# The last projection's last 128 positions with exchanged operands, in a planned two-layer decoder on one core

## The chip, the core and the metric

The kernel runs on one core of a Trainium2 chip. Time is device time of that core in microseconds (us). The core has a matrix engine (TensorE: PE in the profile, PEld for its weight loads), a vector engine (DVE), an activation engine (ACT), a general engine (POOL) and a sync engine (SP), which here issues most DMAs; ACT issues some. Each engine works its own list in order, and waits on semaphores for the others.

## The reference

The model has width 1024, 2048 positions, two layers. What matters here is the end of the second layer and the final norm:

```python
x = x + (o * jax.nn.silu(g)) @ w_out_b[j]      # o: attention, 512 wide; w_out_b: 512 x 1024
return _rmsnorm(x, norm_f)                     # y = x * rsqrt(mean(x*x) + eps) * norm_f
```

Ahead of it stand a gated short-convolution layer, a shared key/value projection and a causal stick-breaking attention with 8 heads of 64. All of it is computed to float32 accuracy.

## The kernel before

Activations are kept transposed, channels on the 128 partitions and positions along a row: the input is `xT`, the output `outT`. The 2048 positions are worked in four chunks of 512 (`CH`), and the kernel's order of positions is reversed. Products of float32 accuracy are made of three faster ones: each operand is split into a high and a low part (`split`), and hi·hi, hi·lo and lo·hi are added up in PSUM (`mm3`). The first layer and the shared projections use a seven-product block scheme (`fast_unit`; tiles `fa`, `fd`, `fe`), the attention (`attend`) scores a band of 192 keys per 128 queries (`z`), takes a sigmoid (ACT), a mask (POOL) and a running product (DVE, a scan, `R`), transposes on PE (`wt`), splits (`wth` on ACT, `wtl` on DVE) and multiplies with the values (`av`). A second, full attention stands behind a flag and a branch at the end of the program, and is not executed for these inputs.

The last stage of a chunk c is `out_kept` for c = 0, 1, 2, and `out_last` for c = 3. The gated attention output of the chunk is `og` (4 tiles of 128 channels, hi and lo); the weights `wob` (w_out_b, hi and lo) stay in SBUF for all four chunks. For each of 8 blocks of 128 output channels (`ob`), 12 products with a block of `wob` as the stationary operand and 512 positions of `og` as the moving one make `pob`, 128 channels by 512 positions; DVE adds the residual `x` (loaded from `x1_d`), ACT squares it, and ACT multiplies by the final gain. In the last chunk the squares of blocks 0 to 4 are added on POOL (`acc`), those of blocks 5 to 7 stay apart; `add_sums` adds all up over the channels with products by a column of ones (`pst`, one column of PSUM for each 128 positions, a full float32 product). Twelve small DVE operations on four columns (`rsqrt`; tiles `v`, `t`, `yr`) make the reciprocal root, four transposes each (`bcast`; tiles `prb_x` and, for POOL, `prb_x23s`, copied to `pbs`) spread it over the partitions, and eight multiplications (six DVE, two POOL) of 128x512 are followed by eight DMAs of 256 KB to `outT`.

Nothing of the order is left to the compiler. The body is recorded (`Recorder`), each operation with its part's name, then put in one order by `order`: a list scheduler with fixed costs for each operation, which takes at each step the operation that can start first, and among equals the one with the smaller key. The keys come from the table `PLAN`: a part's name and the two ends of a stretch of due times (`m..` first layer, `po..` its output, `kq..`/`vg..` the shared projections, `aCH` attention of chunk C and head H, `gCB` the gating, `wo` the loading of `wob`, `oC`/`nC` the last projection and the norm of chunk C). So each engine's list is a result of that table. `square_into`, `rsqrt`, `bcast`, `fold_gains` (splits w_out_b once and writes it to DRAM), `keep_ob` (loads `wob`), `mm3`, `out_b` (branch not taken) and `out_last` are the places that the change touches.

## Time and profile before

| | |
|---|---|
| median of 3 runs | 1340.01 us (1339.97 to 1340.18) |
| the profiled execution | 1341.83 us, of which the profile's span holds 1340.0 us |
| PE busy / weight loads / DVE / ACT / POOL | 1302.8 / 1078.0 / 1016.9 / 599.7 / 435.5 us |
| DMA | 364.99 MB, mean 272 GB/s |
| last product of the last projection (`pob`) ends, by the chain | 1320.87 us |
| last column sum (`pst`) starts | 1324.5 us |
| last output DMA issued | 1332.5 us |

Times within the profile count from the span's start. A line number L363 (L365 after the change) is that of the function which emits the recorded operations, so all rows carry it, and the tile names tell them apart; numbers at the ends of names are left out by the profile (`x` stands for any residual tile, `og_t`, `og_b` and so on are parts of names). "Idle before" is how long the engine stood still just ahead of a group, with the engine that ended it.

### The profile page before, as it was taken

The numbers are of one execution on the slowest core, as the hardware profiler recorded it, in microseconds if no ns is written. First come the engines' busy times: TensorE is split into PE (matmuls) and PEld (weight loads), VectorE is DVE, ScalarE is ACT, GpSimd is POOL, SyncE is SP. The second block draws the span as 40 slices with busy tenths as digits, with TensorE's granted clock in tenths as the row PEclk, the third lists the DMA queues.
The fourth block names the chain that finished last, engine by engine and source line by source line (L and its number), as shares of the span: only waits on it lengthen the run. The fifth ranks groups of instructions, "written<-read, shape, count | busy, mean of one in ns | idle before, by whom it ended". The sixth has DMA issues, their size and how long they took to land.

```text
span 1340.0 us, 18973 instructions
## 1 busy us (share of the span) xinstructions
PE 1302.8 (97%) x6184; PEld 1078.0 (80%) x6184; DVE 1016.9 (76%) x1607; ACT 599.7 (45%) x1052; POOL 435.5 (33%) x553
## 2 busy tenths in 40 slices
PE   8999999999999999999999989999999999999996
PEld 6888888888888888888787777788778887788885
DVE  7899866689964655656869578877998886797855
ACT  7344534444432332323334334554555553566643
POOL 5252000001000000010032355334357675547982
PEclk9999999999999999999999999999999999999997
DMA  9439879878898799987998976887687567999734
GB/s 326 170 130 326 283 271 325 282 278 295 306 355 289 253 356 330 325 289 244 352 322 314 310 260 209 266 264 236 223 301 255 185 209 227 335 367 300 264 106 159
DMA packets 215292, 364.99 MB, mean 272 GB/s; under 512 B 16996, under 2 KB 101008, under 8 KB 215184
## 3 DMA queue, kind: packets, MB, share of 16 engines
q1 hardware_dynamic: 214464, 362.61, 79.4%
q8 instruction: 51, 0.84, 0.2%
q10 hardware_dynamic: 592, 1.05, 0.2%
q14 instruction: 57, 0.47, 0.1%
q0 software_dynamic: 128, 0.02, 0.0%
HBM read 217.35 MB, written 146.28 MB: 271 GB/s over the span
## 4 chain that ended last, share of the span: by engine, by line
PE 78%; DVE 12%; issue 4%; DMA 2%; POOL 2%; ACT 1%; SPq 0%; DVEq 0%; POOLq 0%; ACTq 0%
PE fa_C L363 11%; PE fa_B L363 10%; PE fa_o L363 6%; PE fd_C L363 6%; PE pob L363 5%; PE fd_B L363 5%; PE fa_kq L363 5%; PE fa_vg L363 4%; PE fe_C L363 3%; PE fd_vg L363 3%; PE fe_B L363 3%; PE fd_o L363 3%; PE fd_kq L363 3%; PE av L363 2%; PE wt L363 1%
## 5 line engine op out<-in xcount | busy, mean ns | idle before, releaser
L363 POOL COPY halo<-p 128x2 f32<-128x2 f32 x32 | 15.1, 472 | 435.2 <-DVE p L363 435.2
L363 POOL TENSOR_TENSOR acc_x<-acc_x,sq_x 128x512 f32<-128x512 f32 x53 | 75.4, 1427 | 132.0 <-ACT sq_x L363 127.4
L363 PE MATMUL pob<-og,wob 128*128 128x512 f32 x384 | 103.8, 403 | 0.6 <-DVE x L363 0.6
L363 PE MATMUL fa_C<-op_t,whl_s_C 128*128 128x512 f32 x336 | 83.3, 389 | 0.0
L363 PE MATMUL fa_B<-op_t,whl_s_B 128*128 128x512 f32 x336 | 82.4, 390 | 0.2 <-ACT f_B L363 0.2
L363 PEld LDWEIGHTS pob<-og,wob 128*128 128x128 f32 x384 | 67.6, 189 | 11.9 <-DVE x L363 1.1
L363 DVE TENSOR_TENSOR_SCAN R<-R,ones 128x192 f32<-128x192 f32 x128 | 74.2, 620 | 3.3 <-POOL R L363 3.2
L363 PEld LDWEIGHTS fa_B<-op_t,whl_s_B 128*128 128x128 f32 x336 | 62.9, 188 | 13.6 <-ACT f_B L363 0.6
L363 PEld LDWEIGHTS fa_C<-op_t,whl_s_C 128*128 128x128 f32 x336 | 63.0, 188 | 13.1
L363 DVE SCALAR_TENSOR_TENSOR cv<-p,cols_of,cv 128x512 f32<-128x512 f32 x64 | 50.2, 785 | 11.0 <-ACT cv L363 9.9
L363 ACT ACTIVATE sq_x<-x 128x512 f32<-128x512 f32 x56 | 35.1, 631 | 42.8 <-DVE x L363 32.1
L363 ACT ACTIVATE cv<-p,cols_of 128x512 f32<-128x512 f32 x32 | 23.2, 725 | 68.8 <-DVE p L363 68.8
L363 ACT CAST wth<-wt 128x512 fp32r<-128x512 f32 x64 | 36.4, 574 | 37.5 <-PE av L363 21.5
L363 DVE TENSOR_TENSOR wtl<-wt,wth 128x512 fp32r<-128x512 f32 x64 | 42.4, 667 | 12.4 <-ACT wth L363 11.6
L363 PE MATMUL wt<-ident,R 128*128 128x128 f32 x248 | 46.4, 274 | 1.0 <-DVE R L363 1.0
L363 PE MATMUL fa_C<-op_b,whl_a_C 128*128 128x512 f32 x168 | 43.1, 390 | 0.0
L363 PE MATMUL fa_B<-op_t,whl_a_B 128*128 128x512 f32 x168 | 43.0, 389 | 0.0
L363 PE MATMUL fe_B<-op_b,whl_a_B 128*128 128x512 f32 x168 | 42.9, 390 | 0.0
L363 POOL TENSOR_SCALAR_AFFINE_SELECT R<-R 128x256 f32<-128x256 f32 x64 | 34.9, 552 | 24.6 <-ACT R L363 24.3
L363 PE MATMUL fd_C<-op_t,whl_s_C 128*128 128x512 f32 x168 | 42.3, 390 | 0.1
L363 PE MATMUL fe_C<-op_b,whl_a_C 128*128 128x512 f32 x168 | 42.0, 389 | 0.0
L363 PE MATMUL fd_C<-op_b,whl_s_C 128*128 128x512 f32 x168 | 41.7, 390 | 0.0
(1019 smaller groups left out, 3807.5 us busy)
## 6 DMA issues: line engine op xcount, KB each, us to landing
sw_s_C<-whl_s_C SPq DMA_DIRECT2D x32, 512.0 KB, 4.3
sw_s_B<-whl_s_B SPq DMA_DIRECT2D x32, 512.0 KB, 4.4
q<-q_d SPq DMA_DIRECT2D x32, 512.0 KB, 5.8
sw_a_C<-whl_a_C SPq DMA_DIRECT2D x24, 512.0 KB, 3.5
sw_a_B<-whl_a_B SPq DMA_DIRECT2D x24, 512.0 KB, 3.6
whl_s_C<-sw_s_C SPq DMA_DIRECT2D x24, 512.0 KB, 5.4
whl_s_B<-sw_s_B SPq DMA_DIRECT2D x24, 512.0 KB, 5.4
whl_s_o<-sw_s_o SPq DMA_DIRECT2D x24, 512.0 KB, 5.6
```

Source lines behind the costliest of these rows:

```text
L363: getattr(o.engine.engine, o.name)(*map(real, o.args), **{k: real(v) for k, v in o.kw.items()})
```

## The change

Chunk 3 is the last, and its last 128 columns are now worked the other way round. `out_last` does the 8 blocks as before, but on 384 columns (`n = CH - P`), with the column sums over three blocks of 128. For the last 128 columns the 128 positions of `og` become the stationary operand and 512 output channels of `wob` the moving one: two banks `last_0` and `last_1` of 128 positions by 512 channels, 12 products each, after the blocks. The residual's last 128 columns are turned by eight PE transposes (`pt`) and two ACT copies into `turned`; DVE adds `last` to it. ACT squares and adds up along the row in one operation (`accum_out`), so each position's sum is a column, with no product by ones. The reciprocal root of it (`rsqrt` on one column) scales an identity matrix (`dg`, DVE); eight float32 products with `turned` as stationary and `dg` as moving operand turn the result back and apply the root (`back`); eight copies of 128x128 with the final gain (four ACT, four DVE) fill `done`, and two DMAs of 256 KB write it, one on SP and one on ACT. The norm of the first 384 columns is now part `n3` (five multiplications on DVE, three on POOL, 128x384), and the rest part `le`.

For that, `wob` is kept by half of the channels and by block of 128 inputs (8 tiles of 128 x 2 x 512, as many bytes as before) instead of by output block; `fold_gains`, `keep_ob`, `out_b` and `mm3_ob` follow. The recorder learns that `accum_out` is written. The due times of the parts from the end of the shared projections on are replaced.

```diff
-    "vg22": (1127.46, 1137.33), "kq23": (1116.22, 1131.34), "vg23": (1064.52, 1090.33), "wo": (1281.05, 1315.59),
+    "vg22": (1127.46, 1137.33), "kq23": (1116.22, 1131.34), "vg23": (1064.52, 1090.33), "wo": (1263.07, 1367.8),
...
-    "n2": (1218.33, 1322.06), "o3": (2272.7, 2273.2),
+    "n2": (1456.2, 1834.4), "o3": (2579.2, 2849.85), "n3": (1413.59, 1415.36), "le": (1301.17, 2112.05),
...
+    def mm3_ob(ps, ob, og, n=CH, wt=None):
+        i = 0
+        for k in range(4):
+            for w, m in ((0, 0), (0, 1), (1, 0)):
+                b = (wob[ob // 4][k] if wt is None else wt[k])[:, w, (ob % 4) * P:(ob % 4 + 1) * P]
+                nc.tensor.matmul(ps[:, 0:n], b, og[k][:, m, 0:n], start=i == 0, stop=i == 11)
+                i += 1
...
+        turned = sb.tile([P, 2, CH], F32, name="turned", tag="act", bufs=NA)
...
+            if ob % 4 == 0:
+                pt = psum.tile([P, CH], F32, name=f"pt_{c}_{ob}", tag="av", bufs=NAV)
+            nc.tensor.transpose(pt[:, (ob % 4) * P:(ob % 4 + 1) * P], x[:, n:CH], ident)
+            if ob % 4 == 3:
+                nc.scalar.copy(turned[:, ob // 4, :], pt)
             ps = psum.tile([P, CH], F32, name=f"pob_{c}_{ob}", tag=tag, bufs=bufs)
-            mm3(ps, wob[ob:ob + 1], og_t[c], kt=4)
+            mm3_ob(ps, ob, og_t[c], n)
...
-            nc.vector.tensor_add(x, x, ps)
+            nc.vector.tensor_add(x[:, 0:n], x[:, 0:n], ps[:, 0:n])
...
-        while late:
-            add_sums(late.pop(), False, not late)
-        y = rsqrt(ps2, f"x2{c}")
-        pb = bcast(y, f"x2{c}")
+        ends = []
+        for half in range(2):
+            ps = psum.tile([P, CH], F32, name=f"last_{half}", tag=("lin", "z")[half], bufs=(NLIN, NZ)[half])
+            ends.append(ps)
+            i = 0
+            for k in range(4):
+                for w, m in ((0, 0), (0, 1), (1, 0)):
+                    nc.tensor.matmul(ps, og_t[c][k][:, m, n:CH], wob[half][k][:, w, :], start=i == 0, stop=i == 11)
+                    i += 1
+                if late:
+                    add_sums(late.pop(), False, not late)
+            if half == 0:
+                assert not late
+                y = rsqrt(ps2, f"x2{c}", n=3)
+        nc.part = "n3"
+        pb = bcast(y, f"x2{c}", n=3)
...
-            if k in (2, 6):
-                nc.gpsimd.tensor_mul(x2[k], x2[k], pbs)
+            if k in (1, 3, 6):
+                nc.gpsimd.tensor_mul(x2[k][:, 0:n], x2[k][:, 0:n], pbs[:, 0:n])
...
+        nc.part = "le"
+        sums = const.tile([P, 2], F32, name="sums")
+        for half in range(2):
+            row = turned[:, half, :]
+            nc.vector.tensor_add(row, row, ends[half])
+            sq = sb.tile([P, CH], F32, name=f"sq_last_{half}", tag="q2", bufs=2)
+            nc.scalar.activation(sq, row, AF.Square, accum_out=sums[:, half:half + 1])
+        total = sb.tile([P, 4], F32, name="total", tag="sv")
+        nc.vector.tensor_add(total[:, 0:1], sums[:, 0:1], sums[:, 1:2])
+        y = rsqrt(total, "last", n=1)
+        dg = sb.tile([P, P], F32, name="dg", tag="q2", bufs=2)
+        nc.vector.tensor_scalar(out=dg, in0=ident, scalar1=y, scalar2=None, op0=ALU.mult)
+        done = sb.tile([P, 2, CH], F32, name="done", tag="act", bufs=NA)
+        for half in range(2):
+            ps = psum.tile([P, CH], F32, name=f"back_{half}", tag=("lin", "z")[half], bufs=(NLIN, NZ)[half])
+            for j in range(4):
+                nc.tensor.matmul(ps[:, j * P:(j + 1) * P], turned[:, half, j * P:(j + 1) * P], dg, start=True, stop=True)
+            for j in range(4):
...
+                if j % 2:
+                    nc.vector.tensor_scalar(out=done[:, half, blk], in0=ps[:, blk], scalar1=gains["f"][:, ob:ob + 1], scalar2=None, op0=ALU.mult)
+                else:
+                    nc.scalar.activation(done[:, half, blk], ps[:, blk], AF.Copy, scale=gains["f"][:, ob:ob + 1])
+            (nc.scalar if half else nc.sync).dma_start(
...
```

Up to the middle of the shared projections of chunks 2 and 3 every engine's list is the same as before. Three places show how the lists change behind that. In a row, `out<-in` are tiles, then the shape, and how often.

**PE, the end of the program.** Before: the last block, the four groups of column sums over the four blocks of 128 columns, and the spreading of the root.

```order
L363 MATMUL pob_7_13132<-og_2_12714,wob_11715 128x512 x3
L363 MATMUL pob_7_13132<-og_3_13029,wob_11715 128x512 x3
L363 MATMUL pst_x_13154<-ones,acc_x_13062 128x1 x4
L363 MATMUL pst_x_13154<-ones,sq_x_13143 128x1 x4
L363 MATMUL pst_x_13154<-ones,sq_x_13156 128x1 x4
L363 MATMUL pst_x_13154<-ones,sq_x_13167 128x1 x4
L363 MATMUL prb_x_13193<-ident,yr_x_13182 128x128 x4
L363 MATMUL prb_x23s<-ident,yr_x_13182 128x128 x4
```

Now, from the first product of the last half on:

```order
L365 MATMUL last_13193<-wob_0_11565,og_0_12706 128x512 x3
L365 MATMUL last_13193<-wob_1_11579,og_1_12784 128x512 x3
L365 MATMUL pst_x_13134<-ones,sq_x_13199 128x1 x3
L365 MATMUL last_13193<-wob_2_11632,og_2_12859 128x512 x3
L365 MATMUL last_13193<-wob_3_11687,og_3_13018 128x512 x3
L365 MATMUL prb_x_13237<-ident,yr_x_13218 128x128 x3
L365 MATMUL prb_x23s<-ident,yr_x_13218 128x128 x3
L365 MATMUL back_13280<-dg,turned 128x128 x4
L365 MATMUL back_13288<-dg,turned 128x128 x4
```

The column sums stand six products ahead of the last product instead of behind it, and eight float32 products that need `dg` stand at the end.

**DVE, the end of the program.** Before: the last residual additions, the last steps of the root and the multiplications of all 512 columns.

```order
L363 TENSOR_TENSOR x_3_3_13042<-x_3_3_13042,pob_6_13107 128x512
L363 TENSOR_TENSOR x_3_3_13042<-x_3_3_13042,pob_7_13132 128x512
L363 TENSOR_SCALAR v_x_13178<-pst_x_13154 128x4
L363 TENSOR_SCALAR t_x_13180<-v_x_13178 128x4
L363 TENSOR_SCALAR yr_x_13182<-t_x_13180 128x4
```

Now, from the end of the first root on:

```order
L365 SCALAR_TENSOR_TENSOR yr_x_13218<-t_x_13216,yr_x_13218 128x3
L365 TENSOR_TENSOR total<-sums 128x1
L365 TENSOR_SCALAR v_last<-total 128x1
L365 TENSOR_SCALAR t_last<-v_last 128x1
L365 TENSOR_SCALAR yr_last<-t_last 128x1
L365 TENSOR_TENSOR x_3_0_12940<-x_3_0_12940,prb_x_13237 128x384
L365 TENSOR_TENSOR x_3_1_12965<-x_3_1_12965,prb_x_13237 128x384
L365 TENSOR_TENSOR x_3_2_13001<-x_3_2_13001,prb_x_13237 128x384 x2
L365 TENSOR_TENSOR x_3_3_13029<-x_3_3_13029,prb_x_13237 128x384
L365 TENSOR_TENSOR t_last<-yr_last 128x1
L365 SCALAR_TENSOR_TENSOR t_last<-t_last,v_last 128x1
L365 SCALAR_TENSOR_TENSOR yr_last<-t_last,yr_last 128x1
```

The second root is cut in two by the five multiplications of the first 384 columns; nine of its steps, `dg` and four copies stand behind them.

**PE, attention next to the last shared projection.** Before: two heads of chunks 2 and 1 (`z_7`, the scores; `wt_7`, the transposes of `R_7`).

```order
L363 MATMUL z_7_0_11171<-kt_7_11038,q_2_7_11062 128x192 x4
L363 MATMUL z_7_1_11179<-kt_7_11038,q_2_7_11062 128x192 x4
L363 MATMUL z_7_1_11188<-kt_7_10833,q_1_7_10873 128x192 x4
L363 MATMUL wt_7_0_11212<-ident,R_7_0_11177 128x128
L363 MATMUL wt_7_1_11214<-ident,R_7_0_11177 128x128
L363 MATMUL z_3_0_11217<-kt_3_11114,q_2_3_11102 128x192
L363 MATMUL wt_7_0_11212<-ident,R_7_0_11177 128x128 x2
```

Now the place where transposes follow their scores most closely, another head of chunk 2, further on in the list:

```order
L365 MATMUL z_5_0_11791<-kt_5_11662,q_2_5_11645 128x192 x4
L365 MATMUL z_5_1_11801<-kt_5_11662,q_2_5_11645 128x192 x4
L365 MATMUL pob_4_11728<-og_3_10989,wob_3_11687 128x512 x3
L365 MATMUL pob_5_11830<-og_0_11216,wob_0_11565 128x512 x3
L365 MATMUL wt_5_0_11836<-ident,R_5_0_11799 128x128
L365 MATMUL wt_5_1_11838<-ident,R_5_0_11799 128x128
L365 MATMUL pob_5_11830<-og_1_10994,wob_1_11579 128x512
```

Eight score products stood between the first head's scores and its transposes; now, at the closest, four score products and six of the projection's.

More of the change, by code (lines that the diff above doesn't have):

```diff
@@ L201, in do @@
         o.deps, o.bases = set(), []
+        also = kw.get("accum_out")
         for v in [out] + rest:
@@ L204, in do @@
                 continue
+            wrote_here = v is out or v is also
             b, box = v.base, v.extent()[2]
@@ L209, in do @@
                 for u, wrote, x in b.users:
-                    if (wrote or v is out) and u is not o and box[0] <= x[1] and x[0] <= box[1] and box[2] <= x[3] and x[2] <= box[3]:
+                    if (wrote or wrote_here) and u is not o and box[0] <= x[1] and x[0] <= box[1] and box[2] <= x[3] and x[2] <= box[3]:
                         o.deps.add(u)
-            b.users.append((o, v is out, box))
+            b.users.append((o, wrote_here, box))
     def cost(self, o, out, rest):
@@ L500, in rstd_bcast, with square_into @@
         return bcast(rstd(acc, nm), nm)
-    def square_into(acc, src, first, nm, eng=nc.vector, home=("t", NT)):
+    def square_into(acc, src, first, nm, eng=nc.vector, home=("t", NT), n=CH):
         if first:
@@ L1247, in out_b @@
         for ob in range(KD):
-            wts = load_ob(c, ob)
+            if ob % 4 == 0:
+                wt = []
+                for k in range(4):
+                    wt.append(sb.tile([P, 2, CH], F32R, name=f"wob{c}_{ob}_{k}", tag="whl", bufs=NWB))
+                    nc.sync.dma_start(out=wt[k].bitcast(F32), in_=ob_d[ob // 4][k])
             ps = lin(f"pob_{c}_{ob}")
-            mm3(ps, wts, og, kt=4)
+            mm3_ob(ps, ob, og, wt=wt)
             x = sb.tile([P, CH], F32, name=f"x1o_{c}_{ob}", tag="og", bufs=KD)
@@ L1266, in out_norm @@
             nc.sync.dma_start(out=outT[k * P:(k + 1) * P, cols(c)], in_=t)
-    wob, x2_t = [], {}
+    wob, x2_t = [[], []], {}
     def keep_ob():
-        for ob in range(KD):
-            t = sb.tile([P, 2, Q, P], F32R, name=f"wob_{ob}", tag="act", bufs=NA)
-            nc.sync.dma_start(out=t.bitcast(F32), in_=split_d["ob", ob][0])
-            wob.append(t)
+        for half in range(2):
+            for k in range(4):
+                t = sb.tile([P, 2, CH], F32R, name=f"wob_{half}_{k}", tag="act", bufs=NA)
+                nc.sync.dma_start(out=t.bitcast(F32), in_=ob_d[half][k])
+                wob[half].append(t)
     def gate_kept(c, k, ot):
@@ L1328, in out_last @@
     def out_last(c):
+        n = CH - P
         x2 = x2_rows(c)
@@ L1334, in add_sums @@
         def add_sums(t, first, last):
-            for j in range(4):
+            for j in range(3):
                 nc.tensor.matmul(ps2[:, j:j + 1], t[:, j * P:(j + 1) * P], ones[:, 0:1], start=first and j == 0,
-                                 stop=last and j == 3, skip_group_check=True)
+                                 stop=last and j == 2, skip_group_check=True)
         late = []
+        turned = sb.tile([P, 2, CH], F32, name="turned", tag="act", bufs=NA)
+        pt = None
         for ob in range(KD):
@@ new lines, in out_last @@
+        nc.part = "le"
+        sums = const.tile([P, 2], F32, name="sums")
+        for half in range(2):
+            row = turned[:, half, :]
[4 more added lines that the diff above has]
+        nc.vector.tensor_add(total[:, 0:1], sums[:, 0:1], sums[:, 1:2])
@@ new lines, in out_last @@
+        y = rsqrt(total, "last", n=1)
+        dg = sb.tile([P, P], F32, name="dg", tag="q2", bufs=2)
+        nc.vector.tensor_scalar(out=dg, in0=ident, scalar1=y, scalar2=None, op0=ALU.mult)
+        done = sb.tile([P, 2, CH], F32, name="done", tag="act", bufs=NA)
+        for half in range(2):
+            ps = psum.tile([P, CH], F32, name=f"back_{half}", tag=("lin", "z")[half], bufs=(NLIN, NZ)[half])
+            for j in range(4):
+                nc.tensor.matmul(ps[:, j * P:(j + 1) * P], turned[:, half, j * P:(j + 1) * P], dg, start=True, stop=True)
+            for j in range(4):
+                ob = 4 * half + j
+                blk = slice(j * P, (j + 1) * P)
+                if j % 2:
[3 more added lines that the diff above has]
+            (nc.scalar if half else nc.sync).dma_start(
+                out=outT[4 * half * P:4 * (half + 1) * P, S - CH * c - P:S - CH * c].rearrange("(k p) n -> p k n", p=P),
+                in_=done[:, half, :].rearrange("p (k n) -> p k n", k=4))
```

35 lines of the change are left out of this document (17 added, 18 removed), and 24 rows, old and new, of the table PLAN.

## The prediction

> **What bounds the kernel now.** First the chain of waits over the last 30 us, in order of time (start, us, what):
>
> ```profile
> 1312.66 8.21 PE pob L363 x36
> 1320.87 3.97 PE pst_x L363 x32
> ...
> 1324.86 0.17 DVE v_x L363
> ...
> 1327.03 0.17 DVE yr_x L363
> 1327.34 1.10 PE prb_x L363 x4
> ...
> 1328.53 0.70 DVE x L363
> ```
>
> PE sets the time until 1324.84; behind that stands a serial end. The column sums alone are 3.97 us in which PE does nothing else, the root takes 1324.86 to 1327.20 on DVE (12 operations, 0.195 us apart), its spreading 1.19 us until DVE can start.
>
> Then the end by windows (stretch, its length, busy time of PE, PEld, DVE, ACT, POOL, granted clock, DMA share, GB/s):
>
> ```profile
> 1330.00:1331.00 1.00, 0.00 (x0) 0.00 (x0) 1.00 (x3) 0.00 (x0) 1.00 (x1) 0.50 0.94 334
> 1334.00:1335.00 1.00, 0.00 (x0) 0.00 (x0) 0.00 (x0) 0.00 (x0) 0.00 (x0) 0.50 1.05 395
> 1336.00:1337.00 1.00, 0.00 (x0) 0.00 (x0) 0.00 (x0) 0.00 (x0) 0.00 (x0) 0.50 0.15 45
> 1337.00:1337.40 0.40, 0.00 (x0) 0.00 (x0) 0.00 (x0) 0.00 (x0) 0.00 (x0) 0.50 0.07 26
> ```
>
> The eight output DMAs (2 MB) keep all 16 DMA engines full from 1330 to 1335.7, and stragglers run until 1337.4, while every compute engine is done by 1332.5. From the last data to the span's end go 2.6 us. So 19.1 us pass from the last product of the projection (1320.87) to the end (1340.0).
>
> Last, PE ahead of that, the same view in four stretches, and what its longest waits are:
>
> ```profile
> 1095.00:1110.00 15.00, 13.59 (x69) 10.73 (x68) 14.29 (x18) 7.58 (x14) 10.19 (x10) 1.00 0.68 216
> 1110.00:1165.00 55.00, 55.00 (x272) 46.00 (x271) 35.16 (x52) 24.99 (x47) 29.87 (x40) 1.00 0.84 275
> 1165.00:1175.00 10.00, 7.74 (x54) 6.42 (x53) 9.65 (x19) 5.85 (x12) 4.80 (x14) 1.00 1.02 353
> 1175.00:1320.00 145.00, 143.41 (x850) 123.25 (x849) 111.95 (x203) 86.86 (x155) 103.42 (x148) 1.00 0.73 253
> ```
> ```profile
> 1108.00 0.45 PE L363 MATMUL av<-wtl,vv 128*128 128x256 f32 x2 [1.20 <-DVE wtl L363]
> ...
> 1169.35 0.44 PE L363 MATMUL wt<-ident,R 128*128 128x128 f32 x2 [0.75 <-DVE R L363]
> 1170.42 0.33 PE L363 MATMUL z<-kt,q 128*128 128x192 f32 x1 [0.63 <-DMA kt<-k_d]
> ...
> 1172.07 0.39 PE L363 MATMUL av<-wth,vv 128*128 128x256 f32 x1 [0.35 <-ACT wth L363]
> ...
> 1173.10 0.39 PE L363 MATMUL av<-wtl,vv 128*128 128x256 f32 x1 [0.22 <-DVE wtl L363]
> ```
>
> PE stands still for 1.41 + 0 + 2.26 + 1.59 = 5.3 us between 1095 and 1320: all that a new order can win there, while it can lose more. Five waits make 3.15 us of it.
>
> **Term 1: when PE is through with the last projection.** A 512-column product takes 8.21 / 36 = 0.228 us. A 256-column one, from these starts, 0.12:
>
> ```profile
> 1173.32 0.28 PE L363 MATMUL av<-wth,vv 128*128 128x256 f32 x1
> 1173.44 0.29 PE L363 MATMUL av<-wtl,vv 128*128 128x256 f32 x1
> ```
>
> For 384 columns, not in the trace, I take the middle, 0.174, as the time of the two goes with the columns. 96 x 0.228 = 21.9 us becomes 96 x 0.174 + 24 x 0.228 = 22.2: +0.3. Eight transposes of `x` come in at 0.11 us each, by the row below (+0.9), and the column sums move in front of the last product, 24 of 3.97 / 32 = 0.124 us (+3.0).
>
> ```profile
> 1312.22 0.44 PE prb_x L363 x4
> ```
>
> So the last product of the projection ends 4.2 us later, at 1325.0, if nothing waits. The transposes put the loads of `x` into PE's queue; POOL's multiplications for chunk 1, whose tiles these loads reuse, also stand earlier in the new order, so I count no wait. Without that cover the loads, issued from 1302.7 on in five, landing 4.6 us later, would hold PE by some 2 us.
>
> ```profile
> 1302.72 4.86 SPq L363 DMA_DIRECT2D x<-x_d  x5
> ```
> ```profile
> x<-x_d SPq DMA_DIRECT2D x7, 256.0 KB, 4.6
> ```
>
> **Term 2: from the last product (E) to the end.** Durations from these rows:
>
> ```profile
> 1328.53 3.67 DVE L363 TENSOR_TENSOR x<-x,prb_x 128x512 f32<-128x512 f32 x6 [1.34 <-PE prb_x L363]
> ```
> ```profile
> L363 ACT ACTIVATE x<-x,cols_of 128x512 f32<-128x512 f32 x4 | 2.8, 715 | 0.1
> L363 ACT ACTIVATE sq_x<-x 128x512 f32<-128x512 f32 x2 | 1.2, 614 | 0.0
> L363 PE MATMUL prb_x23s<-ident,yr_x 128*128 128x128 f32 x4 | 1.1, 418 | 0.0
> ```
> ```profile
> DMA to landing us min/median/max: 2.5/3.9/5.4
> ```
>
> 1. DVE adds `last_1` (0.6), ACT squares it (0.61), with 0.2 for handing over: E + 1.5. Meanwhile the root of the 384 columns, begun six products (1.4 us) before E and broken into by that addition, takes 2.35 + 0.6: E + 1.6.
> 2. `total` and three steps, 4 x 0.195: E + 2.4; PE's six transposes and the first result, about 1.0 us behind the root: E + 2.8.
> 3. Five multiplications of 384 columns: 3.67 / 6 = 0.61 for 512, 0.47 by columns: E + 5.1. The 1.5 MB of outputs start to flow at about E + 4 and need 4.2 us at 370 GB/s, with stragglers E + 9.8: not last.
> 4. The nine steps left, 1.75; `dg`, 0.25 (between 0.17 for one column and 0.61 for 512): E + 7.1.
> 5. Eight float32 products. One of these is two PE instructions, as 16 sums make 32 rows; at the half clock, which the windows show granted from 1324 on, instructions follow each other by 1.06 / 5, about 0.21: 16 x 0.21 = 3.4, and 0.3 at both ends: E + 10.8. Below: at the full clock, 16 x 0.124 = 2.0. Above: if a float32 product of 128 columns takes twice the time of one of a single column, 6.8. I take 3.4, as transposes of 128 columns at the half clock keep the same distance.
> 6. The last copy 0.3 (of 0.72 for 512): E + 11.1. The last DMA starts with empty engines: 2.8, near the minimum of 2.5; then 2.6: E + 16.5.
>
> 1325.0 + 16.5 = 1341.5: the exchange itself costs 1.5 us. It trades a DMA-bound end for a longer serial one.
>
> By the Trainium skill, FP8 and Floating Point Precision, section TensorE Precision Notes, a true float32 product makes four passes through the array; the sums here show two instructions, and no row here shows how long one of 128 columns takes. By four passes at a distance of 0.21 each, step 5 would be 6.8, the upper bound, which is a rival below.
>
> By the Trainium skill, TensorE: Matmul & The Clock Gate, section What's actually happening, the clock is halved after an idle window of about 3.4 us and needs as long a busy one to come back; that speaks against the change, as `back` comes 7 us after the last dense work. The windows agree: 0.50 from 1324 on. At the full clock the sum would be 1.4 less.
>
> **Term 3: the new order.** In the old one the transposes of a head stood 8 score products (8 x 1.56 / 12 = 1.0 us, by the row below) behind their scores, and PE waited 0.75 there; so the way over ACT, POOL and DVE takes about 1.7 us at best. In the new one the closest pair has four score products and six of 0.228, 1.9 us, and in front of its scans DVE has an addition that waits for the values' product just ahead: I count 0.6 there, and 0.3 for one `wtl` that follows its transposes closely.
>
> ```profile
> 1167.04 1.56 PE L363 MATMUL z<-kt,q 128*128 128x192 f32 x12
> ```
>
> The wait at 1108 came of DVE:
>
> ```profile
> 1102.90 1.55 DVE L363 TENSOR_TENSOR khl<-f_kq,khl 128x512 fp32r<-128x512 f32 x1
> 1104.38 1.52 DVE L363 TENSOR_TENSOR qhl<-f_kq,qhl 128x512 fp32r<-128x512 f32 x1
> 1105.82 1.52 DVE L363 TENSOR_TENSOR whl_s_kq<-fr_a_kq,whl_s_kq 128x512 fp32r<-128x512 f32 x1
> 1107.27 0.68 DVE L363 TENSOR_TENSOR wtl<-wt,wth 128x512 fp32r<-128x512 f32 x1
> ```
>
> Of the three ahead of `wtl`, two are left there in the new list: 1.5 us less. All five waits should go (-3.15), 0.9 comes: -2.2. Ends: -4 (only 1.3 of idle time is left, as in the stretch without any) and +1.5 (a wait of the kind in rival 2). The loads of `wob` now come by blocks of inputs, so four must be there for the first output block; they also stand earlier in SP's list, and I count nothing for them. The larger pieces of w_out_b's first load are far from any bound.
>
> **Sum:** 1340.0 + 1.5 - 2.2 = 1339.3 us of span; the span of 1340.0 stands beside a median of 1340.01, so the median too is predicted at 1339.3.
>
> **The rivals.**
> 1. *The order wins nearly all.* 1341.5 - 4.3 = 1337.2, and below with a cheaper step 5. For it: the five waits have a cause that the new lists don't repeat. Against it: DVE is busy for 9.65 of 10 us around 1170; who loads it so finds a new wait. 0.23.
> 2. *A wait on DVE takes the place of those removed* (slower): at the closest pair DVE has a queue as at 1168.74, six scans and two `wtl`, 3.12 + 1.27 = 4.4 us, against 1.9 of cover, plus what the scan itself needs: 3.6 us. 1339.3 + 3.6 = 1342.9. It decides from a queue of about 4 us on. Against it: the new list has only two additions there. 0.15.
>
> ```profile
> 1168.74 3.12 DVE L363 TENSOR_TENSOR_SCAN R<-R,ones 128x192 f32<-128x192 f32 x6 [0.35 <-POOL R L363]
> ...
> 1172.37 1.27 DVE L363 TENSOR_TENSOR wtl<-wt,wth 128x512 fp32r<-128x512 f32 x2
> ```
>
> 3. *The float32 products take twice as long:* 1339.3 + 3.4 = 1342.7. For it, their 128 columns; against it, the distance of the transposes. 0.09.
> 4. *The change doesn't do what it says: the order neither wins nor loses, so the exchange alone shows:* 1341.5. 0.08.
>
> **How the numbers follow.** The forecast, 1339.3, has 0.45; its own range is 1337.5 to 1341.2 (terms 2 and 3 off by 1 each way or so). What a measurement can tell from no change is about 0.2%, 2.7 us. Faster than 1337.3: half of rival 1 and its lower part, some of the forecast: 0.25. Slower than 1342.7: most of rival 2, half of rival 3: 0.18. The same: 0.57. The range for 8 in 10 reaches to rival 1 with a little more, and to rival 2: 1336.5 to 1342.9.
>
> **What would show it.** Right: `last_1` ends near 1323 (1325.0 - 2.2); from its end to the span's end 16 to 17 us; `back` for 3.4 us at a clock of 0.50; the last `done` DMA alone on the queues, and PE idle for under 4 us between 1095 and 1320. Wrong: step 5 at 2 or 7 us, output DMAs still full when `done` is issued, PE waiting for `x` at `pt`, or for `R` at a new place by more than 2 us.

## The result and the profile after

The changed kernel took 1344.13 us (median of 10 runs, 1343.01 to 1346.15), the kernel before 1341.46 us (10 runs, 1339.44 to 1343.49). The ratio of the timed runs is 1.0024, with a 95% interval of 1.0014 to 1.0034: slower, by about 3.2 us by that ratio and 2.7 us by the medians. I had forecast 1339.3 us, 0.7 us less than before.

The two profiled spans, 1340.0 and 1341.2 us, show only 1.2 us of that. PE's list is the same in both kernels until about 1047 us, so each span can be cut at one product that stands in both, by the wait ahead of it. On PE's timeline, before:

```profile
1020.69 0.45 PE L363 MATMUL av<-wtl,vv 128*128 128x256 f32 x2 [0.26 <-DVE wtl L363]
```

and after:

```profile
1018.85 0.45 PE L365 MATMUL av<-wtl,vv 128*128 128x256 f32 x2 [0.25 <-DVE wtl L365]
```

The changed kernel's profiled execution was 1.84 us ahead at a place where nothing is changed. All kernels of this document have the same PE list up to there and reach it between 1018.85 and 1022.25, so that is a difference between executions. I therefore count from this product (T0) to the end (E) of the last product of the last projection, and from E to the span's end. Before: 300.18 + 19.13 us (E = 1320.87, by the chain that the prediction shows). After: 302.79 + 19.56 (E = 1321.64). The sum grew by 3.04 us, which agrees with the 3.2 of the ratio. I had forecast +2.0 for the first part and -2.6 for the second; the second is where the forecast broke.

The chain of waits behind E, after (start, us, what):

```profile
1319.59 0.56 PE pst_x L365 x6
1320.15 1.50 PE last L365 x6
...
1323.99 2.41 DVE x L365 x5
1326.40 0.45 DVE t_last L365
...
1326.87 0.93 DVE t_last L365
...
1327.82 0.17 DVE yr_last L365
...
1329.18 0.30 DVE dg L365
...
1329.52 1.66 PE back L365 x6
...
1331.21 0.38 ACT done L365
...
1331.63 2.09 PE back L365 x8
...
1333.74 0.38 ACT done L365
...
1334.16 0.81 PE back L365 x2
...
1335.00 0.36 DVE done L365
...
1335.38 0.38 ACT done L365
...
1335.78 0.35 DVE done L365
```

POOL's multiplications of the first 384 columns, which are not in this chain, run meanwhile; on POOL's timeline:

```profile
1324.87 2.90 POOL L365 TENSOR_TENSOR x<-x,pbs 128x384 f32<-128x384 f32 x3 [14.39 <-ACT pbs L365]
```

Two things are to be seen. Two of the last root's small steps (`t_last`) take 0.45 and 0.93 us, where the others take 0.17; they are the ones that fall before 1327.8, while POOL works. And the last part is a ladder: PE makes six instructions of `back`, waits for an ACT copy, makes eight, waits for an ACT copy again; the copies go ACT, DVE, ACT, DVE, each behind the other. Sixteen instructions and eight copies, which I had priced at 4.0 us, take from 1329.52 to 1336.13, 6.6 us.

PE ahead of E, after, in the stretches that the prediction shows of before (columns as there):

```profile
1095.00:1110.00 15.00, 14.62 (x73) 11.61 (x72) 12.80 (x19) 6.89 (x13) 11.05 (x9) 1.00 0.72 238
1110.00:1165.00 55.00, 55.00 (x288) 46.59 (x287) 38.95 (x54) 26.61 (x50) 30.84 (x42) 1.00 0.81 280
1165.00:1175.00 10.00, 10.00 (x69) 9.10 (x69) 9.78 (x18) 6.34 (x13) 5.88 (x17) 1.00 0.99 373
1175.00:1320.00 145.00, 141.27 (x862) 122.78 (x861) 114.10 (x202) 88.12 (x159) 104.30 (x144) 1.00 0.71 244
```

PE stands still for 0.38 + 0 + 0 + 3.73 = 4.1 us, against 5.3 before (in the later runs with this order 4.0 to 4.8, the longest wait being the same). The stretches at 1095 and 1165 were cleaned, as forecast; behind them stand new waits, the longest three of which are, on PE's timeline:

```profile
1180.64 0.44 PE L365 MATMUL wt<-ident,R 128*128 128x128 f32 x2 [0.57 <-DVE R L365]
...
1274.33 0.45 PE L365 MATMUL av<-wtl,vv 128*128 128x256 f32 x2 [1.19 <-DVE wtl L365]
...
1287.03 0.35 PE L365 MATMUL p_left<-some,ones 128*128 128x1 f32 x2 [0.53 <-DVE some L365]
```

### The profile page after: what moved, and what is told of

The parts are those of the page before. It is cut to its first block, busy times and chain, and to the rows that moved or that the text cites. A ratio compares the mean times of both kernels' runs of the same rounds, so it can differ in the third digit from the quotient of the medians.

```text
span 1341.2 us, 19087 instructions
## 1 busy us (share of the span) xinstructions
PE 1305.6 (97%) x6222; PEld 1082.7 (81%) x6222; DVE 1026.6 (77%) x1626; ACT 601.9 (45%) x1062; POOL 443.6 (33%) x554
## 4 chain that ended last, share of the span: by engine, by line
PE 79%; DVE 12%; POOL 3%; issue 3%; ACT 2%; DMA 1%; SPq 0%; DVEq 0%; POOLq 0%; ACTq 0%
PE fa_C L365 11%; PE fa_B L365 10%; PE fa_o L365 6%; PE fa_kq L365 6%; PE fd_C L365 6%; PE fa_vg L365 5%; PE fd_B L365 5%; PE pob L365 3%; PE fd_vg L365 3%; PE fe_C L365 3%; PE fd_kq L365 3%; PE fd_o L365 3%; PE fe_B L365 3%; PE av L365 2%; PE fe_vg L365 1%
## 5 line engine op out<-in xcount | busy, mean ns | idle before, releaser
L365 POOL TENSOR_TENSOR acc_x<-acc_x,sq_x 128x512 f32<-128x512 f32 (+1 forms) x53 | 75.8, 1434 | 121.8 <-ACT sq_x L365 121.0
L365 PE MATMUL pob<-og,wob 128*128 128x512 f32 (+1 forms) x384 | 103.6, 397 | 0.5 <-DVE x L365 0.5
L365 DVE TENSOR_TENSOR_SCAN R<-R,ones 128x192 f32<-128x192 f32 x128 | 79.3, 657 | 2.0 <-POOL R L365 1.8
L365 PEld LDWEIGHTS fa_C<-op_t,whl_s_C 128*128 128x128 f32 x336 | 63.0, 188 | 13.1
L365 ACT ACTIVATE sq_x<-x 128x512 f32<-128x512 f32 (+1 forms) x56 | 34.4, 617 | 45.7 <-DVE x L365 34.1
```

The costliest lines, as they stand in the source:

```text
L365: getattr(o.engine.engine, o.name)(*map(real, o.args), **{k: real(v) for k, v in o.kw.items()})
```

## The experiments

In the table, T0 to E and E to the end (us) are cut as above; the last column is the ratio of the timed runs with its interval. A row is one profile, and T0 to E differs by 1.1 us among the six later runs whose PE list is the changed kernel's up to E (303.0 to 304.1), so a sum is good to about 1 us; before was profiled once. The texts behind it say what was changed in each; "before" and "the change" are the two kernels themselves.

| run | T0 to E | E to end | sum against before's 319.3 | time against before (95%) |
|---|---|---|---|---|
| before | 300.2 | 19.13 | | |
| the change | 302.8 | 19.56 | +3.0 | 1.0024 (1.0014 to 1.0034) |
| new due times, old end | 305.9 | 18.76 | +5.3 | 1.0045 (1.0027 to 1.0062) |
| old due times, new end | 314.5 | 17.87 | +13.1 | 1.0093 (1.0077 to 1.0109) |
| copies apart | 303.8 | 17.24 | +1.7 | 1.0009 (0.9999 to 1.0020) |
| last root first | 303.6 | 18.31 | +2.6 | 1.0022 (1.0011 to 1.0034) |
| POOL later in the list | 303.0 | 19.64 | +3.3 | 1.0029 (1.0017 to 1.0040) |
| that and copies apart | 303.0 | 17.88 | +1.6 | 1.0006 (0.9995 to 1.0017) |
| the same with PE kept busy | 303.0 | 16.39 | +0.1 | 0.9996 (0.9985 to 1.0006) |
| turned back before the root | 302.6 | 17.95 | +1.2 | 1.0013 (1.0001 to 1.0025) |
| POOL held by data | 303.3 | 18.58 | +2.6 | 1.0010 (1.0001 to 1.0020) |
| POOL held, copies apart | 304.1 | 17.82 | +2.6 | 1.0010 (1.0001 to 1.0019) |
| turned back before the root, POOL held | 304.2 | 15.74 | +0.7 | 1.0003 (0.9994 to 1.0012) |
| turned back before the root, first root earlier | 305.5 | 12.92 | -0.9 | 0.9981 (0.9968 to 0.9995) |

My theory after the result was: the exchange ahead of E cost what I said, the new order won little, and the end failed by two prices that I had left out, the copies' and products' taking of turns and something that slows DVE's small steps. The rivals stand in the expectations.

**The new due times on the old end.**

```diff
 PLAN = {
-    ... "o3": (2272.7, 2273.2),
+    ... (all due times of the changed kernel, for the parts that both have)
```

> The kernel before with the changed kernel's due times, and nothing else of the change; PE's list is the changed kernel's for some 660 more instructions than before's was, and alike behind that. Theory A (the new order wins little: in the changed kernel PE stands still 4.1 us between 1095 us and its last projection product, 5.3 before, and the rest of what it seemed to win stood ahead of 1095, where nothing changed): idle of 3.5 to 5 us there, and 0.3 to 1.8 us less time than before, ratio 0.9987 to 0.9998. Rival B (the order wins the 3 to 4 us that I forecast as its most, and the new end takes them back): idle under 2 us, ratio below 0.998. Rival C (this order fits only the new end): slower than before by over 1 us.

Slower by 6 us: rival C. By the traces PE's list was the changed kernel's for some 740 more instructions than before's (until 1186 us), and up to 1175 the profile is alike (no wait but one of 0.39 us). Behind that the old end's tiles do not fit the times. On this run's timeline of PE:

```profile
1192.73 0.96 PE L363 MATMUL pob<-og,wob 128*128 128x512 f32 x3 [1.14 <-DVE x L363]
...
1208.61 0.41 PE L363 MATMUL wt<-ident,R 128*128 128x128 f32 x2 [0.73 <-DVE R L363]
1209.77 0.44 PE L363 MATMUL wt<-ident,R 128*128 128x128 f32 x2 [0.75 <-DMA q<-q_d]
```

So this run doesn't price the order by itself; it shows that a table of due times belongs to one program, and that part of what Term 3 calls the order can't be had without the rest. For the size of the order's gain I rely on the idle time of the changed kernel alone, 4.1 us in place of 5.3.

**The old due times on the new end.**

```diff
 PLAN = {
-    "wo": (1263.07, 1367.8), ... "o3": (2579.2, 2849.85), "n3": (1413.59, 1415.36), "le": (1301.17, 2112.05),
+    "wo": (1281.05, 1315.59), ... "o3": (2272.7, 2273.2), "n3": (1413.59, 1415.36), "le": (1301.17, 2112.05),
```

> The changed kernel with the due times of before, for all parts but the two new ones. Theory A: the new end's work on PE ahead of its last projection product is 3.3 us, behind that product it is 0.4 us longer than before's 19.1, and the order stays as it was: 3 to 4.5 us above before, ratio 1.0022 to 1.0034, and PE idle of 4.5 to 6 us from 1095 on. Rival B (the new order is worth 3 us or more): over 5.5 us above before, ratio over 1.004.

12.5 us slower, far outside theory A's 3 to 4.5. This is rival B by its number, but not by its reason, since the end was put together anew, with the last projection's blocks waiting for `acc` and `og`. What it costs is more than the waits. By windows of 3.4 us of this run (the stretch, its length, busy us and instructions of PE, PEld, DVE, ACT and POOL, granted clock, DMA share, GB/s):

```profile
1306.00:1309.40 3.40, 3.28 (x19) 2.96 (x18) 0.00 (x0) 0.00 (x0) 3.40 (x4) 1.00 0.73 248
1309.40:1312.80 3.40, 1.55 (x10) 1.17 (x10) 1.38 (x4) 0.26 (x1) 3.03 (x3) 1.00 0.99 349
1312.80:1316.20 3.40, 2.99 (x11) 2.74 (x12) 2.63 (x12) 0.55 (x2) 0.00 (x0) 0.64 0.92 311
1316.20:1319.60 3.40, 3.40 (x20) 3.37 (x19) 3.10 (x6) 2.34 (x5) 1.01 (x1) 0.86 0.40 149
```

Two waits take PE's busy time in one stretch down to 1.55 of 3.4 us (they are 0.94 us, in the row below, and 1.42 us at 1313.21), and the granted clock falls to 0.64 and 0.86 in the next two. In shorter stretches it is 1.00 until 1313, 0.50 from 1314 to 1317, and 0.91 in the next one. What PE did between the two waits was mostly sums of one column:

```profile
1310.22 1.05 PE L365 MATMUL pst_x<-ones,acc_x 128*128 128x1 f32 x8 [0.94 <-POOL acc_x L365]
```

Both runs together say that the new end needed a table of its own, not that the new order gained anything against before.

**The copies apart.**

```diff
-            for j in range(4):
-                if j % 2:
-                    nc.vector.tensor_scalar(out=done[:, half, blk], in0=ps[:, blk], ...)
-                else:
-                    nc.scalar.activation(done[:, half, blk], ps[:, blk], AF.Copy, ...)
+        for half, (ps, behind) in enumerate(backs):      # all eight products stand ahead
+            for j in range(4):
+                if half:
+                    nc.vector.tensor_scalar(out=done[:, half, blk], in0=ps[:, blk], ...)
+                else:
+                    nc.scalar.activation(done[:, half, blk], ps[:, blk], AF.Copy, ...)
```

> The changed kernel with the eight products of the last step all ahead of their copies, and the four copies of a half on one engine (ACT for the first, DVE for the second), not in turn. Theory A (PE's products and the two engines' copies take turns on one bank of PSUM, 0.46 us of waiting twice on PE and 0.43 to 1.27 between the copies): the products take 16 x 0.26 = 4.2 us in place of 5.4 with no wait among them, the last copy ends 5.7 us behind the first product in place of 6.6, and the span is 0.9 us (0.5 to 1.3) shorter than the changed kernel's, ratio to before 1.0014 to 1.0022. Rival B (the clock and the two instructions for each product hold PE, the waits are covered): products 5 us or more, no gain.

On this run's timelines of PE and, in the second block, of DVE (start, us, engine, line, operation, tiles, shapes, how many, and in brackets the wait ahead):

```profile
1322.33 1.63 PE L365 MATMUL last<-wob,og 128*128 128x512 f32 x6
...
1331.83 3.42 PE L365 MATMUL back<-dg,turned 128*128 128x128 f32 x16 [5.24 <-DVE dg L365]
```

and DVE:

```profile
1335.30 1.12 DVE L365 TENSOR_SCALAR done<-back,cols_of 128x128 f32<-128x128 f32 x4 [3.52 <-PE back L365]
```

The sixteen instructions run through in 3.42 us (0.21 each), four copies of one engine follow each other at 0.28 us, and the end is 17.24 us behind E: 2.3 us less. Theory A, and more than the 0.9 that it promised: I had counted 0.26 us per instruction, from the ladder, as PE's own pace. Two cautions belong to the 2.3. The granted clock came back to 1.00 at about 1334.6, during the last of these instructions, which it did not in the changed kernel; a run below has the price at one clock. And the edit does two things at once, all products ahead of the copies and one engine for each bank; which of them gives how much was not tried.

**The last root first.**

```diff
+        # part "le" up to dg is recorded ahead of "n3"
             else:
                 nc.vector.tensor_mul(x2[k][:, 0:n], x2[k][:, 0:n], pb[:, 0:n])
+                nc.ops[-1].deps.add(behind)              # dg
```

> The changed kernel with the five multiplications of the first 384 columns on DVE put behind the scaled identity matrix, so that the last root runs without a break. Theory A (the chain of the last root ends the kernel, not the output DMAs): the matrix is ready 2.4 to 3.5 us earlier (near 1326 in place of 1329.5), and the span is 2.3 to 3.5 us shorter than the changed kernel's, ratio to before 0.9998 to 1.0007. Rival B (the output DMAs of the 384 columns, which now start 2.7 us later and flow for 4.2 us, end last): gain under 1 us, the last DMA waits behind them. Rival C (POOL's three multiplications now meet the root's small steps, which took 0.5 and 0.9 us in place of 0.16 while POOL worked): three or more steps over 0.4 us, and half of the gain lost, 1.2 to 1.8 us.

Three steps of the last root in a row on this run's timeline of DVE, and then what POOL does at that time:

```profile
1329.20 0.93 DVE L365 SCALAR_TENSOR_TENSOR yr_last<-t_last,yr_last 128x1 f32<-128x1 f32 x1
1330.16 0.92 DVE L365 TENSOR_TENSOR t_last<-yr_last 128x1 f32<-128x1 f32 x1
1331.11 0.92 DVE L365 SCALAR_TENSOR_TENSOR t_last<-t_last,v_last 128x1 f32<-128x1 f32 x1
```

POOL:

```profile
1329.12 2.89 POOL L365 TENSOR_TENSOR x<-x,pbs 128x384 f32<-128x384 f32 x3 [14.38 <-ACT pbs L365]
```

Rival C: with the root moved, other steps of it are slow, three of them, exactly while POOL's three multiplications run (0.96 us each). POOL's end at 1330.1, 1331.1 and 1332.0, and the slow steps at 1330.13, 1331.08 and 1332.03: each ends with one of POOL's. The end comes 1.25 us earlier (18.31), not 2.3 to 3.5.

**POOL held back.** The first try only moved POOL's multiplications in the list:

```diff
             if k in (1, 3, 6):
                 nc.gpsimd.tensor_mul(x2[k][:, 0:n], x2[k][:, 0:n], pbs[:, 0:n])
+                nc.ops[-1].deps.add(behind)              # dg, for the order of recording alone
```

> The changed kernel with POOL's three multiplications of the first 384 columns held back until the scaled identity matrix is made, so that POOL stands still during the last root. Theory A (POOL's multiplications slow DVE's small steps: they took 0.52 and 0.92 us while POOL worked and 0.16 otherwise): every step of the last root takes 0.15 to 0.17 us, from the last projection product to the matrix pass 6.7 us in place of 7.8, and from that product to the end 18.5 in place of 19.6. Rival B (the two slow steps come of DVE's own five multiplications just ahead, which still drain): the two steps stay at 0.5 and 0.9 us, 19.6.

Nothing moved: POOL had nothing else to do and started as soon as its inputs were there, before the root's steps, as in the changed kernel. On POOL's timeline of this run:

```profile
1327.09 2.90 POOL L365 TENSOR_TENSOR x<-x,pbs 128x384 f32<-128x384 f32 x3 [14.40 <-ACT pbs L365]
```

Its place in the list could not hold POOL back, as nothing else stood ahead of it there; a datum can. The second try made the tile that POOL reads depend on the root:

```diff
+        hold = const.tile([P, 1], F32, name="hold")
+        nc.vector.tensor_scalar(out=hold, in0=y_last, scalar1=0.0, scalar2=1.0, op0=ALU.mult, op1=ALU.add)
-        nc.scalar.copy(pbs[:, 0:n], bcast(y, f"x2{c}s", n=3)[:, 0:n])
+        nc.scalar.activation(pbs[:, 0:n], bcast(y, f"x2{c}s", n=3)[:, 0:n], AF.Copy, scale=hold)
```

(The outputs of POOL's tiles also went to SP, and the DMAs of `done` stand behind them in the order.)

> The changed kernel with POOL's three multiplications really held back: the copy that they read is scaled by a column of ones that DVE makes from the last root, so it can't be there before the scaled identity matrix is made; in the earlier try they had only been moved in the list and ran at the same time as before. Theory A (POOL's multiplications slow DVE's small steps): all steps of the last root take 0.15 to 0.17 us, 6.7 us from the last projection product to the matrix in place of 7.8, 18.5 us to the end. Rival B (the steps are slow because they follow DVE's own multiplications): still one step of 0.5 and one of 0.9 us, 19.6.

The two steps that were slow in the changed kernel, on this run's timeline of DVE:

```profile
1327.70 0.15 DVE L365 TENSOR_TENSOR t_last<-yr_last 128x1 f32<-128x1 f32 x1
1327.88 0.16 DVE L365 SCALAR_TENSOR_TENSOR t_last<-t_last,v_last 128x1 f32<-128x1 f32 x1
```

and POOL's multiplications, which now start behind them:

```profile
1330.54 2.90 POOL L365 TENSOR_TENSOR x<-x,pbs 128x384 f32<-128x384 f32 x3 [18.70 <-ACT pbs L365]
```

Theory A: behind the same five multiplications of DVE the two steps now take 0.15 and 0.16 us, `dg` is ready 6.7 us behind E (7.8 in the changed kernel), and the end comes at 18.58. POOL was the cause of 1.0 us.

**Both.** Without and with the real hold:

> POOL's three multiplications held back behind the scaled identity matrix, and the copies of a half on one engine, behind all eight products. Theory A (those two, the taking of turns at 2.3 us and POOL's share at 1.1, are all that the end had more than I forecast): 16.1 us from the last projection product to the end, within 0.5 of the forecast's 16.5; against before the stretch from the middle of the shared projections to that product is 2.4 us longer, so the sum is 0.6 us below before, ratio 0.9988 to 1.0002. Rival B (the held back outputs of POOL's tiles now end last): 17.5 us or more.

> The same, and the copies of a half on one engine behind all eight products. Theory A: 16.2 us from the last projection product to the end, as the forecast's 16.5, and the whole 0.5 us below before (2.3 more ahead of that product, 2.9 less behind it), ratio 0.9988 to 1.0003. Rival B (the outputs of POOL's tiles, now issued near 10 us behind that product, end last): 17 us or more.

The first is in effect the copies' run again, as POOL wasn't held, so that its 17.88 says nothing of rival B. It is 0.64 us longer than the copies' run, and the sixteen instructions show why in part:

```profile
1330.20 3.78 PE L365 MATMUL back<-dg,turned 128*128 128x128 f32 x16 [5.25 <-DVE dg L365]
```

Here the clock stays at 0.50 for all of them, 0.236 us each. From the first of them to the last copy pass 4.95 us in both of these runs, 6.61 in the changed kernel and in the run with POOL held by data. So at one clock the taking of turns costs 1.7 us; the 2.3 of the copies' run has the clock's return in it.

The second gave 17.82 where theory A asked for 16.2: rival B. The chain did as expected, the last copy ended 11.7 us behind E (14.5 in the changed kernel); but POOL's tiles were now written last, and their 0.6 MB flowed together with `done`. By windows of the second run (the last two columns are the DMA share and GB/s):

```profile
1333.00:1336.00 3.00, 2.82 (x14) 2.52 (x12) 0.14 (x1) 1.14 (x4) 2.71 (x3) 0.50 0.27 92
1336.00:1339.00 3.00, 0.00 (x0) 0.00 (x0) 0.99 (x4) 0.00 (x0) 0.00 (x0) 0.50 0.91 283
```

So the two prices are each shown alone (1.7 us at one clock, and 1.0), but the end that has neither was not reached in a run. The 16.2 of the expectation is a sum with the 2.3 in it; this run's 11.7 and the 5.1 that the changed kernel needs behind its last copy give 16.8, a sum too.

**PE kept busy.** The run with both in its first form, and products that nobody reads:

```diff
+        keep_busy(7, at_end)        # behind the last projection product
...
+        keep_busy(17, at)           # behind the first root's spreading
```

> As the run with both, and 7 products of 512 columns that nobody reads on PE right behind the last projection product, and 17 more between the spreading of the first root and the last step's products, so that PE hardly stands still. Theory A (the last step's products go at half the clock only because PE stood still for over 3.4 us): the granted clock stays at 1.00, the sixteen instructions take 2.0 us in place of 3.4, and from the last projection product to the end pass 14.8 us. Rival B (two instructions of a float32 product follow each other at 0.21 us at any clock): 3.4 us again, 16.1. Rival C (the added products run into the last step): the products begin over 0.3 us behind the matrix.

The sixteen instructions on PE's timeline of this run:

```profile
1331.96 2.05 PE L365 MATMUL back<-dg,turned 128*128 128x128 f32 x16 [1.44 <-DVE dg L365]
```

Theory A: 2.05 us in place of 3.78 in the run without, at a granted clock of 1.00, and the end at 16.39 in place of 17.88. (It says 14.8 in the expectation since POOL was thought to be held.) PE still waited 1.44 us for `dg`, and the clock stayed.

**Turned back before the root.** If the end is a chain, the product with `dg` and its copies need not be in it: eight plain transposes of `turned` can run before the root is known, ACT copies them with the gain, and the root is applied at the very end.

```diff
-        dg = ...; nc.tensor.matmul(ps[:, ...], turned[:, half, ...], dg, start=True, stop=True)
+            nc.tensor.transpose(ps[:, j * P:(j + 1) * P], row[:, j * P:(j + 1) * P], ident)   # behind each half's addition
+        pl = bcast(y_last, "last", n=1)
+            nc.vector.tensor_mul(four, four, pl[:, 0:P].unsqueeze(1).to_broadcast([P, 4, P]))
```

> The changed kernel with the last 128 columns turned back by eight plain transposes before the root is known, four of them before the last projection product; ACT copies them with the final gain while DVE works on the root; then one transpose spreads the root and two DVE multiplications of 512 columns apply it. The last root runs first, and all eight multiplications of the first 384 columns behind it. Theory A (the end is a serial chain, and the product with the scaled matrix and its copies, 6.6 us, need not be in it): root ready 4.1 us behind the last projection product, last DVE multiplication at 7.9 us, end at 13.0 us (12.5 to 14); with 2.6 us more ahead of that product than before, 3.5 us under before, ratio 0.9965 to 0.9982. Rival B (the output DMAs, 2 MB within 6 us, become the bound): end at 14.9 us or more, ratio 0.9985 to 0.9995.

> The version that turns the last columns back before the root is known, with POOL held back by data until the root is made, and POOL's tiles written from ACT, all others from SP. Theory A: steps of 0.16 us, root ready 4.0 us behind the last projection product (6.4 in the first try), last DVE multiplication at 7.9 us (9.8), end at 13.3 us (12.7 to 14.2) in place of 18.0; 3.3 us under before as a whole, ratio 0.9968 to 0.9985. Rival B (2 MB of outputs within 5 us are then the bound, at some 370 GB/s 5.7 us from 4.7 us on, with stragglers of 1.7 us and 2.7 us to the end): 14.8 us or more, ratio over 0.9985.

The first form met POOL: three steps of 0.92 to 0.96 us, 17.95 to the end. With POOL held the chain was as expected, DVE done at 1332.62, 7.8 us behind E, but the end came at 15.74: rival B in its reason. All outputs now start behind the root, and by windows of the second run the queues are the bound:

```profile
1330.00:1331.00 1.00, 0.15 (x1) 0.00 (x0) 1.00 (x4) 0.00 (x0) 1.00 (x2) 0.63 0.56 204
1331.00:1336.00 5.00, 0.00 (x0) 0.00 (x0) 1.62 (x3) 0.00 (x0) 1.76 (x2) 0.50 1.02 340
1336.00:1337.00 1.00, 0.00 (x0) 0.00 (x0) 0.00 (x0) 0.00 (x0) 0.00 (x0) 0.50 0.80 239
```

**And the first 384 columns out of the way.** The last version lets their root and outputs go ahead of the end:

```diff
+        if c == 2:                                  # chunk 2's multiplications give way to chunk 3's addition
+            nc.part = "n2m"                         # due last; two of the eight on POOL
...
-            (nc.scalar if k % 2 else nc.sync).dma_start(out=outT[...], in_=x2[k][:, 0:n])
+            nc.sync.dma_start(out=outT[...], in_=x2[k][:, 0:n])
```

> As the version that turns the last columns back before the root is known, but the first 384 columns get out of the way ahead of the end: of chunk 2's last eight multiplications two go to POOL (behind a copy on ACT), the other six give way on DVE to the last residual addition, so that the first root is done some 2 us before the last projection product and is spread between its products; all outputs of the first 384 columns are issued by SP, POOL isn't held back. Theory A (the end is then the serial chain of the last root alone): the last projection product ends 1.1 us later than in the changed kernel (10 transposes in front of it), POOL is through before the last root begins, so that its steps take 0.16 us, and from that product to the end pass 11.6 us (11 to 13); 4 us below before, ratio 0.9960 to 0.9980. Rival B (the outputs, now 3.5 MB between 1313 and 1327 us at some 370 GB/s, still flow when the last two DMAs are issued): 13.5 us or more, ratio 0.998 or more. Rival C (PE stands still at the spreading for the first root): over 0.5 us of waiting there, which comes on top.

Faster than both kernels: 1339.62 us, 0.9981 of before (0.9968 to 0.9995), just short of what theory A asked for. The end is theory A's, 12.92 us behind E and all steps at 0.16 us; it is not the 11.6 expected, since the last addition stands behind the five multiplications in DVE's list and starts only at 1326.82, 1.3 us behind E (0.1 in the changed kernel). Rival C didn't come: PE has no wait from 1318 to E. By windows, the outputs of the 384 columns are out before the last two DMAs start:

```profile
1329.00:1331.00 2.00, 0.09 (x1) 0.12 (x1) 1.45 (x10) 0.39 (x2) 0.00 (x0) 0.62 0.82 275
1331.00:1333.00 2.00, 0.35 (x1) 0.06 (x1) 1.29 (x2) 0.00 (x0) 0.00 (x0) 0.50 0.05 12
1333.00:1335.00 2.00, 0.00 (x0) 0.00 (x0) 0.00 (x0) 0.00 (x0) 0.00 (x0) 0.50 0.87 255
```

E came later than expected (2.7 us more from T0 than in the changed kernel, 1.1 forecast); which of the moved instructions cost that I didn't follow up.

## Why the prediction was wrong, step by step

**Term 1 and Term 3 together** (T0 to E) were forecast at +2.0 and came at +2.6 in the changed kernel's profile, +2.8 to +3.9 in the six later runs with the same PE list up to E. By parts:

- Term 1, +4.2: the transposes cost what I said, and the 384-column products nearly (the chain has eight of them in 1.42 us, 0.178 each against 0.174: 0.4 more for all 96); the loads held nobody up. The column sums take 0.56 / 6 = 0.093 us between other products, not 0.124 as at the end of before: 0.7 less. About +3.8 is left if the order is taken as below.
- Term 3, -2.2: the five waits went, as forecast, -3.15; but 2.0 us of new ones came, not 0.9. I had looked for them at the closest pair of scores and transposes (no wait came there) and not at 1274, where `wtl` is late by 1.19 us. What is left is -1.2 of idle, and only -0.4 in the later run that waits most (4.8).

**Term 2, 16.5 us from E to the end,** measured 19.56. Steps 1 to 3 were right: the second sum is there at E + 1.6 (forecast 1.5 to 1.6), the multiplications start at E + 2.35 (2.8) and end at E + 4.8 (5.1).

- Step 4, forecast 2.0 us for nine steps and `dg`, took 3.08. The step I left out is POOL's three multiplications of 128x384, which run at that time. It is shown by the runs with the last root first and with POOL held by data: the slow steps go where POOL's work goes, and go away without it, 1.0 us in all.
- Steps 5 and 6 up to the last copy, forecast 3.7 + 0.3, took 6.6. My price of 0.21 us for an instruction was nearly right (0.236 at a clock of 0.50, which makes 0.4 us for sixteen); the upper bound and rival 3, twice that, were wrong. What I left out is the wait between products and copies of one bank: I costed eight copies at 0.3 us, as if seven were hidden, and never asked whether PE may write a bank that ACT reads. That is 1.7 us. Even with the copies apart four of them stand behind the last product, not one: 1.17 us from its end to theirs, 0.6 more than I counted.
- The last DMA and the end, forecast 2.8 + 2.6, took 5.07.

3.06 us on Term 2 and 0.6 on the others turn my -0.7 into +3.0. No rival had this mechanism, and none of the signs of being wrong that I had named came: the products of step 5 took 5.4 us with their waits, neither 2 nor 7. Rival 3 has the time, 3.4 us on the last step, but for a reason that the runs rule out. The forecast's median also started from 1340.01, of three runs; the ten runs of before beside the changed kernel have 1341.46, so 1.5 us of the distance between 1339.3 and 1344.13 are of the scale, not of the change.

POOL's price could have been read beforehand. Before's DVE has small steps of the very same kind that take over a microsecond beside POOL's work. On before's timeline of DVE:

```profile
1239.96 1.18 DVE L363 SCALAR_TENSOR_TENSOR t_x<-t_x,v_x 128x4 f32<-128x4 f32 x1
```

POOL at that time:

```profile
1239.81 1.32 POOL L363 TENSOR_TENSOR acc_x<-acc_x,sq_x 128x512 f32<-128x512 f32 x1
```

I took 0.195 us from the root at the end of before, where POOL happened to stand still. The kernel's own scheduler knows this price, too: `cost` marks (`turns`) the operations of DVE, and the larger ones of POOL, with two operands outside PSUM, and `order` starts none while the other engine has a marked one under way. By the Trainium skill, SBUF — State Buffer, section Who interferes with whom, a DVE instruction with two SBUF inputs contends with a GpSimd instruction that reads SBUF, and one with at most one SBUF input outside the two-port modes does not. The traces agree: the root's two-input steps took 0.92 us beside POOL, while DVE's multiplications by `prb_x`, which stands in PSUM, took 0.48 each (2.41 us for five) with POOL at work for over half of that time, and just as long with POOL held. In the run with the old due times on the new end three one-input steps of the last root stood beside POOL's third multiplication (1338.18 to 1338.71) and took 0.15 each. One row does not fit the count of inputs alone: in before a one-input step of four columns took 1.22 us (1235.36) beside POOL; why was not tried.

By the Trainium skill, PSUM — Partial Sum Buffer, section PSUM bank collisions raise a hardware error, no two of TensorE, ScalarE and VectorE may access the same bank in the same 32 partitions at a time, reads included, and the guard has to be by bank and partitions, or simply by bank. The waits of this program are of that kind: PE waits for a copy that reads other columns of the bank, 0.46 us twice, and the copies wait for each other. The ladder of the chain above is the price.

The loss of clock that I did weigh was there: with PE kept busy the last products took 2.05 us at 1.00, and the end came 1.5 us earlier, near the 1.4 that I had set against it. But I read the windows of before wrongly when I said that they agree with an idle window. PE was not idle when the clock fell; it had made nothing but one-column sums since 1320.87 (busy of PE is the first number behind the length, the clock the third from the end):

```profile
1322.00:1323.00 1.00, 1.00 (x11) 1.00 (x11) 0.00 (x0) 0.97 (x3) 0.00 (x0) 1.00 0.00 0
1324.00:1324.50 0.50, 0.50 (x4) 0.50 (x4) 0.00 (x0) 0.00 (x0) 0.00 (x0) 0.50 0.00 0
```

## What to carry to other kernels

Price a serial end not by the durations of its instructions alone but by who else holds their ports and banks at that time: a two-input step of one column beside a busy POOL costs up to six times as much, and copies that go in turn between two engines, out of banks that PE still fills, run at the pace of the ladder. Let one engine empty a bank, after all products for it are through, and let data, not the place in a list, hold back an engine that is otherwise idle. Work that does not need the last value (here the turning back and the gain) belongs ahead of that value, and bulk outputs ahead of the last few.

## What the runs showed of the hardware that I had not expected

- DVE and POOL went in turn, instruction by instruction: while POOL made multiplications of 0.96 us, each two-input DVE step of one column took 0.92 us, three in a row, and each ended with one of POOL's.
- The granted clock fell without a long wait of PE. In before it was 0.50 some 2.8 us after the last dense product, with one-column sums all the way; in the run with the old due times it fell after waits of 0.94 and 1.42 us and 1.55 us of work, most of it such sums. With dense products ahead, a wait of 1.44 us left it at 1.00.
- Executions of one and the same list differ by up to 3.4 us by T0 (1018.85 to 1022.25), which is more than the change itself; a pair of profiles can be compared to better than that only from a common instruction on.
